# Delta rule chain: the state update finished in PSUM by an identity matmul

## Chip, cores and metric

The kernel runs on one core of a Trainium2 chip. The metric is device time of one execution in microseconds (us). The engines are called PE (TensorE, matmul), PEld (its weight loads), DVE (VectorE), ACT (ScalarE), POOL (GpSimd) and SP (SyncE, here the issuer of the DMAs). PSUM is the memory into which PE writes and from which DVE and ACT read.

## The reference, cut to what matters

Four layers; each mixes tokens and then applies a feed-forward block, over 512 tokens (256 of context, 256 latent). Token mixing has two parallel branches. The one that matters here is an RWKV-7 mixer with 8 heads of width 64, in two directions. Its state is a 64x64 matrix per head and direction:

```
sa = -einsum('vk,k->v', S, kk_t)
S  = S * w_t + sa * b_t + v_t * k_t        (decay per key channel, two outer products)
y  = einsum('vk,k->v', S, r_t)
```

The kernel computes it in chunks of 64 tokens. Within a chunk the decay is folded into keys and queries (a key is multiplied by the inverse of the decay so far, a query by the decay so far). From chunk to chunk the state, written with keys on the partitions, becomes `c * (K^T U + S)`. Here `c` is the decay over the whole chunk (one number per key channel), `K` holds the scaled keys and b vectors of the chunk, and `U` holds its values and solved vectors.

## The kernel before, in words

Nothing is emitted as it is written. Each call on `pe`, `act`, `vec`, `pool` or `dma` records a node (`Plan.add`, line 150) with its predecessors and an estimated cost (line 198). `Plan.schedule` (line 243) then orders all nodes of the whole kernel by list scheduling: each engine takes the ready node with the highest rank, and a rank is the estimated length of the longest chain behind the node plus a bias by stream. `emit` (line 338) issues everything in that order from one line, L343, so the profile is read by tile names and not by lines. Calls inside `plan.together(share)` (line 140) become one node and are issued in a row; `share` multiplies their estimated cost. Each engine works through its own instructions in the order issued.

In the mixing stage of a layer several generators (streams) run against each other (lines 1312 to 1337): for each of four head pairs `rw_pair` (preparation, line 812), `rw_solve` (a triangular inverse, line 985) and `rw_chain` (the chunk recurrence, line 1031), for each of four heads of the other branch `hg_head` (line 1140), and `gate_tiles` (line 1300). All of them draw projections through `proj` (line 521): weights are loaded as `wr`, split into two parts by ACT (`wh`) and by DVE or POOL (`wl`), and used in three matmuls into `p_ps`.

`rw_pair` writes, per direction `d` and half `s4` (chunks 0 to 3, then 4 to 7), the keys `BK` (128 partitions: two heads of 64 key channels; 512 columns a half). It takes score matmuls of them (`pz`, masked by DVE into `SC`), transposes them on PE and has ACT copy them into `BKT`. `pcs[:, d, s]` is the decay over chunk `s`, one number per partition.

`rw_chain` runs over chunks `s` = 0 to 7 of a pair; there are four pairs in each of four layers, so 128 steps, 112 of which (`s` < 7) update the state, 96 of them with an old state (`s` > 0). A step is a relay in one PSUM tile, `c_ps`, of which there is one buffer (`PSB`, line 49):

1. four matmuls of `SC` and `UV`, in which the state sits (profile: `c_ps<-UV,SC`), copied out by ACT into a part of the tile `S` (`S<-c_ps`, line 1052);
2. four matmuls by `ZA` (`c_ps<-S,AR`), copied by ACT into `UV` (two instructions, line 1059);
3. four matmuls of `BKT` and `UV` into columns 256 to 383 (`c_ps<-UV,BKT`, line 1066);
4. the state update on DVE (lines 1075 to 1087): for each direction and head into `UV` of the next chunk, 64x64, and for each direction into the tile `S`, 128x64. It reads the PSUM columns, multiplies by `pcs` and adds `S0P`, the old state already multiplied by `pcs` on POOL (line 1072). For `s` = 0 there is no old state, and the instruction only multiplies.

After chunks 2, 3, 6 and 7 outputs `y` are taken from the same PSUM tile (lines 1089 to 1112).

Of the kernel before, what the change touches and what calls it, by code (L numbers as in the profile page):

```python
# [12 lines left out]
AF = mybir.ActivationFunctionType  # L13
ALU = mybir.AluOpType
PSUM = bass.MemoryType.PSUM

P = 128
# [12 lines left out]
C = 64  # L30
# [62 lines left out]
class Plan:  # L93
# [104 lines left out]
    def cost(eng, name, out, args, kw):  # L198
# [31 lines left out]
        if name == "tensor_scalar":  # L230
            if ptr:
# [7 lines left out]
               act=dict(pe=230.0, act=145.0, vec=143.0, pool=170.0, dma=200.0),  # L239
               vec=dict(pe=245.0, act=130.0, vec=127.0, pool=130.0, dma=200.0),  # L240
               pool=dict(pe=205.0, act=72.0, vec=156.0, pool=97.0, dma=200.0))
# [112 lines left out]
def body(ctx, tc, xT, cc, ada_w, w_in, rw_lo, rw_g2, proj_a, proj_b, w_out, ffn_w1, ffn_w2,  # L354
         vecs, lbl, c_id, c_bo, c_sc, c_hg, c_sh, out, depth=4):
    nc = tc.nc
    plan = Plan(nc, tc)
    vec, act, pool, pe, dma = plan.vec, plan.act, plan.pool, plan.pe, plan.dma
# [13 lines left out]
    def st(tag, shape, dt=F32, bufs=1):  # L372
        return plan.tile(sp, shape, dt, tag, 2 if tag in B2 else bufs, tag)
# [6 lines left out]
    ident = const(c_id, name="ident")  # L380
# [17 lines left out]
    def sps(tag="s"):  # L398
        return plan.tile(pss, [P, 512], F32, tag, PSB[tag], tag + "_ps")
# [342 lines left out]
    hd = (slice(0, C), slice(C, P))  # L742

    def layer(l, pm, xs, xd, hh, hl):
# [67 lines left out]
        def rw_pair(p):  # L812
# [116 lines left out]
            for s4 in range(0, NCH, 4):  # L929
                yield lambda s4=s4: p == 0 or flags.get(("chain", p - 1), -1) >= s4 + 3  # L930
                yield ("at", par["ps"][p] + par["pn"])
                ss = slice(s4, s4 + 4)
                for h in range(0 if s4 else 2):
                    pool.memset(UV[hd[h], :, 0, h, :], 0.0)
                w = C if last and s4 == 0 else P
                for d in range(2):
                    BK, ar = BKs[d], ARt[:, d]
                    pz = [sps().rearrange("p (s c) -> p s c", s=4) for _ in range(2)]
                    with plan.together(0.55):
                        for i in range(4):  # L940
                            for h in range(2):
                                pe.matmul(pz[h][:, i, 0:w], BK[hd[h], s4 + i, :, :], ar[hd[h], s4 + i, 0:w // C, :],
                                          start=True, stop=True)
                    for h in range(2):
                        hs, psv = hd[h], pz[h]
                        vec.tensor_tensor(out=SC[:, d, ss, h, 0:w], in0=psv[:, :, 0:w],
                                          in1=scm[:, 0:w].unsqueeze(1).to_broadcast([P, 4, w]), op=ALU.mult)
                        if not EA[last]:
                            vec.tensor_tensor(out=ZA[z0, d, ss, h, :], in0=psv[hs, :, 0:C],
                                              in1=scm[hs, 0:C].unsqueeze(1).to_broadcast([C, 4, C]), op=ALU.mult)  # L950
                        pool.tensor_copy(SC[hs, d, ss, h, 0:C], ar[hs, ss, 0, :])
                        yield 1
                    ps = sps()
                    for i in range(4):
                        pe.transpose(ps[:, i * P:(i + 1) * P], BK[:, s4 + i, :, :], ident)
                    act.activation(BKT[:, d, ss, :], ps.rearrange("p (a c) -> p a c", a=4), AF.Copy)
                    yield 1
                    ps = sps()
                    for i in range(2):
                        o0 = (s4 + 2 * i) * C  # L960
                        pe.transpose(ps[:, i * P:(i + 1) * P], (vr if d else v)[:, o0:o0 + P], ident)
                    for g in range(2):
                        pv = ps[hd[g], 0:2 * P].rearrange("p (a h c) -> p a h c", a=2, h=2)
                        for h in range(2):
                            act.activation(UV[hd[1 - h], d, s4 + g:s4 + 4:2, h, :], pv[:, :, h, :], AF.Copy)
                    yield 1
# [64 lines left out]
        def rw_chain(p):  # L1031
# [12 lines left out]
            for s in range(NCH):  # L1044
                ps = sps("c")
                pu = ps[z0, 0:256]
                with plan.together():
                    for d in range(2):
                        for h in range(2):
                            pe.matmul(pu[:, (2 * d + h) * C:(2 * d + h + 1) * C], SC[:, d, s, h, 0:C],  # L1050
                                      UV[:, d, s, h, :], start=True, stop=True)
                act.activation(Rs, pu, AF.Copy)
                with plan.together():
                    for d in range(2):
                        for h in range(2):
                            pe.matmul(ps[hd[h], d * C:(d + 1) * C], ZA[z0, d, s, h, :],
                                      Rs[:, (2 * d + h) * C:(2 * d + h + 1) * C], start=True, stop=True)
                for h in range(2):
                    act.activation(UV[hd[h], :, s, h, :], ps[hd[h], 0:2 * C].rearrange("p (d c) -> p d c", d=2),
                                   AF.Copy)  # L1060
                yield 1
                if s < NCH - 1:
                    with plan.together():
                        for d in range(2):
                            for h in range(2):
                                pe.matmul(ps[hd[h], 256 + d * C:256 + (d + 1) * C],
                                          BKT[:, d, s, h * C:(h + 1) * C], UV[:, d, s, h, :], start=True, stop=True)
                    s0p = [None, None]
                    if s:
                        for d in range(2):  # L1070
                            s0p[d] = st("S0P", [P, C], bufs=2)
                            pool.tensor_scalar(out=s0p[d], in0=S[:, d, s % 4, :], scalar1=pcs[:, d, s:s + 1],
                                               scalar2=None, op0=ALU.mult)

                    def update(dst, d, r):
                        po, pc = ps[r, 256 + d * C:256 + (d + 1) * C], pcs[r, d, s:s + 1]
                        if s:
                            vec.scalar_tensor_tensor(out=dst, in0=po, scalar=pc, in1=s0p[d][r], op0=ALU.mult,
                                                     op1=ALU.add)
                        else:  # L1080
                            vec.tensor_scalar(out=dst, in0=po, scalar1=pc, scalar2=None, op0=ALU.mult)

                    for d in range(2):
                        for h in range(2):
                            update(UV[hd[h], d, s + 1, h, :], d, hd[h])
                    for d in range(2):
                        update(S[:, d, (s + 1) % 4, :], d, slice(0, P))
                    yield 1
                if s % 4 < 2 or last and s < 4:
                    flags["chain", p] = s  # L1090
                    continue
                ns = (s - 1, s) if s % 4 == 2 else (s - 3, s)
                steps = []
                for i, n in enumerate(ns):
                    sb = 3 - n if n < 4 else 11 - n
                    steps += [(0, i, 0, n), (0, i, 1, sb)] + [(1, i, 0, n)] * (n > 0) + [(1, i, 1, sb)] * (sb > 0)
                steps.sort()
                fin = {i: x for x in steps for i in (x[1],)}
                with plan.together(0.75):
                    for x in steps:  # L1100
                        st_, i, d, n = x
                        for h in range(2):
                            po = ps[hd[h], 384 + i * C:384 + (i + 1) * C]
                            if st_:
                                w, a = S[hd[h], d, n % 4, :], ARt[hd[h], d, n, 1, :]
                            else:
                                w, a = UV[:, d, n, h, :], SC[:, d, n, h, C:P]
                            pe.matmul(po, w, a[:, ::-1] if d else a, start=x == steps[0], stop=fin[i] == x,
                                      skip_group_check=True)
                st_ = ns[1] - ns[0]  # L1110
                act.activation(y.rearrange("p (n c) -> p n c", c=C)[:, ns[0]:ns[1] + 1:st_],
                               ps[:, 384:512].rearrange("p (n c) -> p n c", c=C), AF.Copy)
                flags["chain", p] = s
                yield 1
# [410 lines left out]
```

## Time and profile before

| | |
|---|---|
| median of 3 runs | 4313.35 us (4310.06 to 4324.89) |
| profiled execution, its own time | 4312.55 us |
| span of that execution (first to last instruction) | 4310.8 us |
| busy: PE, PEld, DVE | 3855.0, 3058.9, 3309.3 us |
| busy: ACT, POOL | 2149.9, 1890.7 us |
| mean granted TensorE clock | 0.932 |

A granted clock of 1.00 is TensorE at 2.4 GHz throughout, one of 0.50 at 1.2 GHz throughout. Busy PE time includes matmuls that overlap in its pipeline, so the length of a matmul group on PE is better read from the start of the group to the start of the next one. Matmuls of fp32 operands are recorded as two instructions each. Rows with `x4` merge four instructions into one line of the timeline.

### The profile page before, as it was taken

The numbers are of one execution on the slowest core, as the hardware profiler recorded it, in microseconds if no ns is written. First come the engines' busy times: TensorE is split into PE (matmuls) and PEld (weight loads), VectorE is DVE, ScalarE is ACT, GpSimd is POOL, SyncE is SP. The second block draws the span as 40 slices with busy tenths as digits, with TensorE's granted clock in tenths as the row PEclk, the third lists the DMA queues.
The fourth block names the chain that finished last, engine by engine and source line by source line (L and its number), as shares of the span: only waits on it lengthen the run. The fifth ranks groups of instructions, "written<-read, shape, count | busy, mean of one in ns | idle before, by whom it ended". The sixth has DMA issues, their size and how long they took to land.

```text
span 4310.8 us, 71511 instructions
## 1 busy us (share of the span) xinstructions
PE 3855.0 (89%) x26290; PEld 3058.9 (71%) x26290; DVE 3309.3 (77%) x5764; ACT 2149.9 (50%) x4234; POOL 1890.7 (44%) x1617
## 2 busy tenths in 40 slices
PE   7889998899988998999999889899899997788898
PEld 4666666777776666677777766677777775567798
DVE  5989979999179899668753898987676379988676
ACT  4556653433255566544333555565433255566564
POOL 1343444455433444464554243454455433244332
PEclk8889899999998898999999989899999998788999
DMA  4111137466321111363543212116354331112555
GB/s 150 57 53 48 52 122 217 138 182 177 91 85 52 59 50 55 122 186 115 159 123 107 64 38 63 43 56 221 108 164 140 108 102 45 41 51 63 170 151 160
DMA packets 661407, 451.02 MB, mean 105 GB/s; under 512 B 28224, under 2 KB 584256, under 8 KB 661056
## 3 DMA queue, kind: packets, MB, share of 16 engines
q1 hardware_dynamic: 661056, 446.44, 34.7%
q8 instruction: 207, 3.39, 0.3%
q14 instruction: 144, 1.18, 0.1%
HBM read 416.98 MB, written 29.36 MB: 104 GB/s over the span
## 4 chain that ended last, share of the span: by engine, by line
PE 42%; DVE 19%; issue 10%; POOL 5%; ACT 2%; DMA 1%; POOLq 0%; SPq 0%; DVEq 0%; ACTq 0%
PE p_ps L343 32%; POOL wl L343 4%; PE s_ps L343 4%; DVE XS L343 4%; PE c_ps L343 3%; PE g_ps L343 2%; DVE wl L343 2%; DVE S L343 2%; DVE X8b L343 1%; DVE AR L343 1%; DVE hX L343 1%; DVE UV L343 1%; DVE X8a L343 1%; DVE BK L343 1%; DVE X4c L343 1%
## 5 line engine op out<-in xcount | busy, mean ns | idle before, releaser
L343 PE MATMUL p_ps<-hh,wl 128*128 128x512 f32 (+1 forms) x2784 | 1091.0, 397 | 107.0 <-DVE wl L343 53.5
L343 PE MATMUL p_ps<-hh,wh 128*128 128x512 f32 (+1 forms) x2784 | 1073.9, 390 | 0.0
L343 PE MATMUL p_ps<-hl,wh 128*128 128x512 f32 (+1 forms) x2784 | 1066.2, 389 | 0.0
L343 ACT ACTIVATE wh<-wr 128x512 fp32r<-128x512 f32 x986 | 611.0, 622 | 860.8 <-PE p_ps L343 684.4
L343 POOL TENSOR_TENSOR wl<-wr,wh 128x512 fp32r<-128x512 f32 x487 | 674.3, 1392 | 746.9 <-ACT wh L343 517.0
L343 PEld LDWEIGHTS p_ps<-hh,wl 128*128 128x128 f32 x2784 | 543.7, 196 | 245.9 <-POOL wl L343 77.0
L343 PEld LDWEIGHTS p_ps<-hl,wh 128*128 128x128 f32 x2784 | 541.8, 195 | 97.6 <-issue 7.2
L343 PEld LDWEIGHTS p_ps<-hh,wh 128*128 128x128 f32 x2784 | 543.6, 196 | 90.7 <-issue 4.9
L343 DVE TENSOR_TENSOR wl<-wr,wh 128x512 fp32r<-128x512 f32 (+1 forms) x499 | 377.6, 762 | 99.6 <-ACT wh L343 89.9
L343 POOL TENSOR_SCALAR fn<-fn 128x512 f32<-128x512 f32 (+1 forms) x152 | 236.4, 1555 | 246.1 <-ACT fn L343 220.0
L343 POOL TENSOR_SCALAR S0P<-S,pcs 128x64 f32<-128x64 f32 x192 | 151.4, 802 | 316.8 <-DVE S L343 316.2
L343 DVE TENSOR_TENSOR fn<-fn,p_ps 128x512 f32<-128x512 f32 (+1 forms) x208 | 127.7, 615 | 162.0 <-ACT fn L343 81.2
L343 ACT ACTIVATE fn<-fn 128x512 f32<-128x512 f32 (+1 forms) x304 | 174.5, 575 | 103.2 <-POOL fn L343 98.8
L343 POOL TENSOR_TENSOR HB<-HB,HA 128x512 f32<-128x512 f32 x112 | 157.7, 1408 | 155.2 <-ACT hY L343 153.2
L343 DVE TENSOR_TENSOR XS<-XS,S 64x30 f32<-64x30 f32 (+14 forms) x480 | 203.9, 425 | 11.7
L343 DVE TENSOR_TENSOR S<-XS 64x30 f32<-64x30 f32 (+14 forms) x480 | 193.2, 402 | 11.6
L343 POOL COPY SC<-XS 64x256 f32<-64x256 f32 x128 | 67.6, 528 | 263.1 <-DVE SC L343 250.3
L343 POOL TENSOR_TENSOR HA<-HA 128x512 f32<-128x512 f32 x112 | 144.2, 1287 | 11.4 <-ACT hX L343 5.0
L343 PE MATMUL p_ps<-SC,wh 128*128 128x512 f32 (+1 forms) x440 | 144.2, 361 | 0.0
L343 DVE SCALAR_TENSOR_TENSOR UV<-c_ps,pcs,S0P 64x64 f32<-64x64 f32 x384 | 108.6, 283 | 36.7 <-PE c_ps L343 26.6
L343 ACT ACTIVATE fn<-p_ps 128x512 f32<-128x512 f32 (+1 forms) x217 | 112.2, 518 | 42.9 <-PE p_ps L343 23.6
L343 ACT ACTIVATE hY<-HB 128x512 f32<-128x512 f32 x128 | 85.0, 664 | 89.2 <-PE g_ps L343 74.5
(478 smaller groups left out, 8761.7 us busy)
## 6 DMA issues: line engine op xcount, KB each, us to landing
wr<-ffn_w SPq DMA_DIRECT2D x512, 256.0 KB, 3.1
wr<-w_in SPq DMA_DIRECT2D x408, 256.0 KB, 2.9
hq<-ada_w SPq DMA_DIRECT2D x242, 256.0 KB, 3.0
PB<-ada_w SPq DMA_DIRECT2D x110, 256.0 KB, 2.8
wr<-w_out SPq DMA_DIRECT2D x64, 256.0 KB, 3.0
gts<-fn SPq DMA_DIRECT2D x48, 256.0 KB, 2.4
wr<-proj_a SPq DMA_DIRECT2D x32, 256.0 KB, 3.9
wr<-proj_b SPq DMA_DIRECT2D x32, 256.0 KB, 3.6
```

The lines of the kernel that those rows point to most:

```text
L343: getattr(self.eng[self.on[i]], name)(*args, **kw)
```

## The change

In `rw_pair` one DVE instruction is added per direction and half: after the score matmuls have read the keys, `BK` is multiplied in place by the chunk decay. In `rw_chain` the DVE update goes. POOL still multiplies the old state by the decay, now both directions into one tile with one buffer. PE starts the accumulation with two identity matmuls that bring this tile into PSUM, and the four matmuls with `BKT` add to it. ACT copies the result into `UV` (two instructions), DVE copies it into `S` (one instruction).

```diff
                         pool.tensor_copy(SC[hs, d, ss, h, 0:C], ar[hs, ss, 0, :])
                         yield 1
+                    bk = BK[:, ss].rearrange("p s x j -> p s (x j)")
+                    vec.tensor_tensor(out=bk, in0=bk, in1=pcs[:, d, ss].unsqueeze(2).to_broadcast([P, 4, P]),
+                                      op=ALU.mult)
                     ps = sps()
                     for i in range(4):
                         pe.transpose(ps[:, i * P:(i + 1) * P], BK[:, s4 + i, :, :], ident)
...
                 if s < NCH - 1:
-                    with plan.together():
+                    if s:
+                        s0p = st("S0P", [P, 2, C], bufs=1)
+                        for d in range(2):
+                            pool.tensor_scalar(out=s0p[:, d], in0=S[:, d, s % 4, :], scalar1=pcs[:, d, s:s + 1],
+                                               scalar2=None, op0=ALU.mult)
+                    with plan.together(0.7):
+                        for h in range(2 if s else 0):
+                            pe.matmul(ps[hd[h], 256:256 + 2 * C], ident[:, hd[h]], s0p.rearrange("p d c -> p (d c)"),
+                                      start=True, stop=False, skip_group_check=True)
                         for d in range(2):
                             for h in range(2):
                                 pe.matmul(ps[hd[h], 256 + d * C:256 + (d + 1) * C],
-                                          BKT[:, d, s, h * C:(h + 1) * C], UV[:, d, s, h, :], start=True, stop=True)
-                    s0p = [None, None]
-                    if s:
-                        for d in range(2):
-                            s0p[d] = st("S0P", [P, C], bufs=2)
-                            pool.tensor_scalar(out=s0p[d], in0=S[:, d, s % 4, :], scalar1=pcs[:, d, s:s + 1],
-                                               scalar2=None, op0=ALU.mult)
-
-                    def update(dst, d, r):
-                        po, pc = ps[r, 256 + d * C:256 + (d + 1) * C], pcs[r, d, s:s + 1]
-                        if s:
-                            vec.scalar_tensor_tensor(out=dst, in0=po, scalar=pc, in1=s0p[d][r], op0=ALU.mult,
-                                                     op1=ALU.add)
-                        else:
-                            vec.tensor_scalar(out=dst, in0=po, scalar1=pc, scalar2=None, op0=ALU.mult)
-
-                    for d in range(2):
-                        for h in range(2):
-                            update(UV[hd[h], d, s + 1, h, :], d, hd[h])
-                    for d in range(2):
-                        update(S[:, d, (s + 1) % 4, :], d, slice(0, P))
+                                          BKT[:, d, s, h * C:(h + 1) * C], UV[:, d, s, h, :], start=not s,
+                                          stop=True, skip_group_check=True)
+                    new = ps[:, 256:256 + 2 * C].rearrange("p (d c) -> p d c", d=2)
+                    for h in range(2):
+                        act.activation(UV[hd[h], :, s + 1, h, :], new[hd[h]], AF.Copy)
+                    vec.tensor_copy(S[:, :, (s + 1) % 4, :], new)
                     yield 1
```

## Rows read from the trace of the kernel before

**Rows 1.** Windows: three mixing stages, and the sum over all four.
```profile
100.00:640.00 540.00, 481.79 (x4111) 359.79 (x4111) 480.18 (x925) 313.49 (x633) 220.99 (x217) 0.91 0.21 62
1210.00:1815.00 605.00, 535.29 (x4388) 408.39 (x4388) 532.46 (x1026) 348.53 (x706) 245.96 (x236) 0.90 0.20 61
2330.00:2915.00 585.00, 518.16 (x4263) 399.20 (x4262) 501.13 (x977) 338.44 (x684) 236.24 (x231) 0.91 0.19 58
...
sum 2265.00, PE 1977.97 PEld 1523.81 DVE 1980.95 ACT 1313.63 POOL 919.68; mean PE 494.49 PEld 380.95 DVE 495.24 ACT 328.41 POOL 229.92
```

**Rows 2.** Chain that ended last, 1210 to 1815 us, shares by engine and tile.
```profile
by line: PE p_ps L343 26.5%; issue 9.6%; PE s_ps L343 8.1%; DVE XS L343 8.0%; PE c_ps L343 7.0%; DVE wl L343 5.1%; PE g_ps L343 4.7%; DVE S L343 4.3%; DVE X8b L343 3.2%; DVE AR L343 2.5%; DVE hX L343 2.4%; DVE X8a L343 1.8%; DVE SC L343 1.8
```

**Rows 3.** Groups by shape, DVE: count | busy us, mean ns | idle before, releasers.
```profile
L343 DVE SCALAR_TENSOR_TENSOR UV<-c_ps,pcs,S0P 64x64 f32<-64x64 f32 x384 | 108.6, 283 | 36.7 <-PE c_ps L343 26.6 <-ACT wh L343 2.6 <-ACT he L343 0.6
L343 DVE SCALAR_TENSOR_TENSOR S<-c_ps,pcs,S0P 128x64 f32<-128x64 f32 x192 | 45.6, 279 | 2.2
L343 DVE TENSOR_SCALAR UV<-c_ps,pcs 64x64 f32<-64x64 f32 x64 | 18.1, 283 | 10.0 <-PE c_ps L343 6.6 <-ACT wh L343 2.4
L343 DVE TENSOR_SCALAR S<-c_ps,pcs 128x64 f32<-128x64 f32 x32 | 7.6, 279 | 0.5
```

**Rows 4.** Groups by shape, DVE, the nearest to the added instructions.
```profile
L343 DVE TENSOR_TENSOR SC<-s_ps,scm 128x512 f32<-128x512 f32 x112 | 76.4, 684 | 3.4 <-PE s_ps L343 2.1
...
L343 DVE TENSOR_TENSOR X8a<-X8a,X8b 128x512 f32<-128x512 f32 x32 | 27.6, 864 | 0.2
...
L343 DVE COPY SS<-g_ps 128x128 f32<-128x128 f32 x32 | 8.1, 278 | 3.1 <-PE g_ps L343 3.0
```

**Rows 5.** Groups by shape, ACT, the copy into UV.
```profile
L343 ACT ACTIVATE UV<-c_ps 64x128 f32<-64x128 f32 x256 | 69.1, 270 | 65.9 <-PE c_ps L343 61.4 <-DVE S L343 1.2
```

**Rows 6.** Timeline, one update of the last chain of layer 0: start, length.
```profile
593.37 0.45 PE L343 MATMUL c_ps<-UV,BKT 128*64 128x64 f32 x8
...
593.75 0.50 PE L343 MATMUL p_ps<-hh,wh 128*128 128x512 f32 x1
...
593.97 1.21 DVE L343 SCALAR_TENSOR_TENSOR UV<-c_ps,pcs,S0P 64x64 f32<-64x64 f32 x4 [0.35 <-PE c_ps L343]
594.09 0.60 PE L343 MATMUL g_ps<-vt,HB 128*128 128x128 f32 x4
...
594.45 0.71 PE L343 MATMUL p_ps<-hl,wh 128*128 128x512 f32 x2
...
595.21 0.47 DVE L343 SCALAR_TENSOR_TENSOR S<-c_ps,pcs,S0P 128x64 f32<-128x64 f32 x2
...
595.66 0.85 POOL L343 TENSOR_SCALAR S0P<-S,pcs 128x64 f32<-128x64 f32 x2 [6.13 <-DVE S L343]
...
595.83 0.65 PE L343 MATMUL c_ps<-UV,SC 128*64 128x64 f32 x8
...
598.76 0.45 PE L343 MATMUL c_ps<-UV,BKT 128*64 128x64 f32 x8
```

**Rows 7.** Timeline, one update of the first chain of layer 0.
```profile
236.72 0.64 PE L343 MATMUL c_ps<-UV,BKT 128*64 128x64 f32 x8
...
240.48 1.21 DVE L343 SCALAR_TENSOR_TENSOR UV<-c_ps,pcs,S0P 64x64 f32<-64x64 f32 x4
241.72 0.48 DVE L343 SCALAR_TENSOR_TENSOR S<-c_ps,pcs,S0P 128x64 f32<-128x64 f32 x2
242.10 2.19 POOL L343 TENSOR_SCALAR S0P<-S,pcs 128x64 f32<-128x64 f32 x2 [2.07 <-DVE S L343]
```

**Rows 8.** Tile S0P: ns min/median/max; last, idle time of its engines by releaser.
```profile
L343 POOL TENSOR_SCALAR S0P<-S,pcs x192: 433/542/3309, 233.1 to 4010.4; 128x64 f32<-128x64 f32 x192
...
  PE c_ps L343: 26.6, 29
```

**Rows 9.** Timeline, two readers of one PSUM tile in the last layer's tail.
```profile
4296.92 0.38 ACT L343 ACTIVATE fn<-p_ps 128x256 f32<-128x256 f32 x1 [3.18 <-PE p_ps L343]
...
4297.33 0.48 DVE L343 TENSOR_SCALAR hY<-p_ps,pr 128x256 f32<-128x256 f32 x1 [3.13 <-ACT fn L343]
```

## The prediction

> **What bounds the kernel now.** I began with the table of busy times. PE is busy for 3855.0 of 4310.8 us, but it is not the only limit, so the next view is the windows over the four mixing stages, where all of the change lies [rows 1]. There the reader is to see two engines almost equally full: PE 1978.0 and DVE 1981.0 of 2265 us (87% each), ACT at 58%, POOL at 41%, and a granted clock of about 0.9 (between the levels 1.2 and 2.4 GHz, nearer the higher). Which of two full engines limits such a stage is read from the chain that ended last in it [rows 2]. PE stands there with 26.5 + 8.1 + 7.0 + 4.7 = 46%, DVE with 8.0 + 5.1 + 4.3 + 3.2 + 2.5 + 2.4 + 1.8 + 1.8 = 29% in the lines that are listed, and 25% is left for issue time, hand-overs and small lines. So a microsecond taken off DVE is worth about 0.29 us, one put on PE costs about 0.46 us, and a relay through the chain's steps counts by about 0.25. These three weights are my estimate; one stage stands for all four.
>
> **DVE.** The change removes the whole update: 108.6 + 45.6 + 18.1 + 7.6 = 179.9 us [rows 3]. It adds 112 copies of 128x128 from PSUM. The same shape takes 278 ns, so 31 us [rows 4]. It adds 64 scalings of 128x512 in SBUF (4 pairs, 2 directions, 2 halves, 4 layers). They are not in the trace. The nearest are an fp32 product of the same shape with one operand in PSUM at 684 ns and one with both operands in SBUF at 864 ns [rows 4]: 44 to 55 us, nothing below, since they replace no instruction. I take 55, the operands being in SBUF. Net: -179.9 + 31 + 55 = -94 us, and -107 with the shorter price and 253 ns a copy (8.1 us / 32). At 0.29 that is -27 us. What a lighter DVE leaves late next is the projections and chain matmuls on PE, which have the larger weight already. The scaling stands between score matmuls and transposes. What is queued behind it on DVE is the next mask or the solver; the transposes and ACT's copy into `BKT` wait for it. `BKT` is read only in the third part of a chain step, so I give this wait no price of its own; without that cover the first update of each half waits, 32 halves by 0.86 us, 28 us at weight 0.25, 7 us.
>
> **PE.** In 96 steps two identity matmuls come ahead, fp32, 64 outputs by 128 columns: four recorded instructions. Four instructions of 128 columns take 594.45 - 594.09 = 0.36 us from start to start; the four existing matmuls, eight instructions of 64 columns, 0.38 us [rows 6]. If the two heads, which go to different halves of the array's outputs, overlapped fully it would be half, 0.18. So 17 to 36 us, of which I take 0.36 x 96 = 35, since the group in the trace has the same number of columns. At 0.46 it costs 16 us.
>
> **ACT and POOL.** ACT gains 224 copies of 0.270 us [rows 5], 60 us. What hides them is ACT's free time, 42% of the stages [rows 1]; the part that the chain sees is in the next term. Without that cover the 60 us count like the chain, about 15 us. POOL does the same 192 products as before.
>
> **The relay of a step.** Before, on a free DVE, the next matmuls start 595.83 - 593.37 = 2.46 us after the matmuls of the update: 0.60 to DVE's first instruction, 1.71 of updates, 0.15 back [rows 6]. The output tile has one buffer, so the copy into `S` must end as well. After: 0.36 (identity) + 0.60 + 0.54 (two ACT copies) + hand-over + 0.28 (DVE copy) + 0.15. How DVE and ACT stand to each other decides the hand-over, and [rows 9] shows it: two readers of one PSUM tile with no data between them, and DVE sat idle 3.13 us until ACT had ended, then began 0.03 us later. So 0.36 + 0.60 + 0.54 + 0.03 + 0.28 + 0.15 = 1.96, a gain of 0.50. On a loaded step DVE came only 240.48 - 236.72 = 3.76 us after the matmuls [rows 7], and afterwards two queues, ACT's and DVE's, lie one behind the other, so the gain there may be nothing. I take 0.3 us: 112 x 0.3 x 0.25 = -8 us; the ends are 0 and -14.
> On this the Trainium skill (PSUM — Partial Sum Buffer, section on bank collisions) speaks against the change: two engines must not touch one bank in the same 32 partitions at once, reads included, and compilers put one behind the other. By that rule, which the idle DVE of [rows 9] bears out, the sum stays as above; were the copies side by side, each step would be 0.31 us shorter still.
>
> **Sum.** -27 + 16 - 8 = -19 us against the profiled execution's 4312.55 (span 4310.8 and 1.75 around it), so 4293.5; the median of the runs lies 0.8 above, so 4294.
> The planner orders everything anew, and what an order is worth can be bounded: the three stages that run the same code leave PE idle for 58.2, 69.7 and 66.8 us [rows 1]. A spread of 11.5, so about 6 either way a stage: 12 us over four if independent, 23 if all go one way.
>
> **Rivals.**
> *PE is the bound (slower).* If PE's stretches weigh 0.8 and DVE's 0.1, because PE's queue is in order and its group grows in every step, the sum is +28 - 9 = +19: 4332. For: PE has the largest share [rows 2]. Against: DVE's 29% are stretches in which PE waits. It decides from the point where PE's weight is over 2.7 times DVE's (94 / 35); now it is 1.6.
> *The old state comes late (slower).* Before, the product `S0P` was needed only by DVE's update; DVE's idle time before those was ended by PE, never by POOL [rows 8]. Now PE itself waits for it, and projections and other heads' matmuls are queued behind. The spare time was 598.76 - 596.51 = 2.25 us in a free step [rows 6], but a pair takes 0.85 there, 2.19 in the loaded one [rows 7], and one product has taken 3.31 [rows 8]. If a quarter of the 96 steps lose 1.5 us on PE, that is +36 on -19: +17, 4330. Against: median 542 ns, so most pairs take 1.1 us. It decides from 13 steps on (19 / 1.5).
> The Trainium skill (SBUF — State Buffer, section on the two separate sides) has a rule that feeds this one: a DVE instruction with two SBUF inputs and a POOL instruction that reads SBUF exclude each other for their whole length. The removed updates had one SBUF tensor and the added scaling has two, so by the rule, which the stretch from 433 to 3309 ns agrees with, 64 new blocks reach POOL; I raise this rival from 0.10 to 0.12 for it, no more.
> *Nothing to be measured.* DVE's time is refilled at once because weight splits, solver and projections are late next, and its weight is half of what the chain shows: -14 + 16 - 8 = -6, 4307. For: both engines are equally full. Against: the saving lies in the stretch where DVE makes PE wait.
> *The copies run side by side.* 112 x 0.31 x 0.25 = 9 us and the low end of the identity cost, 8 us less: 4277. Against: [rows 9].
>
> **How the numbers follow.** Forecast 0.45, no change 0.20, PE bound 0.15, old state late 0.12, side by side 0.08. A difference of 0.3% is 13 us, about what a measurement of this kernel can tell from no change: 4300 to 4326. The forecast and its spread by order (4282 to 4306) give 0.37 faster and 0.08 same; side by side 0.08 faster; no change 0.04 faster, 0.14 same, 0.02 slower; the two slower rivals 0.24 slower, 0.03 same. Together: faster 0.49, same 0.25, slower 0.26. The low end takes DVE's net at -107 with a weight of 0.45 (all unlisted lines DVE's), 17 us of PE, 0.5 us a step and a good order: -48 + 8 - 14 - 12 = -66, 4247. The high end is above both slower rivals with a little of the bad order: 4337. The forecast's own range is 4270 to 4306.
>
> **What would show it.** DVE busy about 94 us less in all, ACT 60 more; the identity group 0.36 us from its start to the group with `BKT`; DVE's copy into `S` beginning just after ACT's second copy into `UV`; few PE idles ended by POOL `S0P`; mixing stages together some 20 us shorter, everything else alike. The prediction is wrong if DVE's lines in the chain shrink and PE's grow by as much, if PE idles for `S0P` add up to over 20 us, or if the stages move by more than the spread of the order while the counts come out as worked out here.

## The result, and the profile after

The changed kernel takes 4346.38 us (median of 4 runs, 4344.15 to 4350.16) where the kernel before took 4316.68 beside it: ratio 1.006, 95% interval 1.0044 to 1.0075. By the ratio it is slower by about 26 us (the two medians lie 30 apart) where 19 less were forecast, and it lies above the range of 4247 to 4337.

The first lines of the page of after (share of the span, instructions), against 4310.8 and PE 3855.0, DVE 3309.3, ACT 2149.9 before:

```profile
span 4343.5 us, 72016 instructions
...
PE 3886.8 (89%) x26674; PEld 3078.2 (71%) x26674; DVE 3187.3 (73%) x5265; ACT 2206.8 (51%) x4458; POOL 1868.0 (43%) x1620
```

PE is busy for 31.8 us more and idle as long as before (span less PE's busy time: 455.8, then 456.7 us), so on balance the lighter DVE has shortened no waiting of PE. The work is what was counted, and DVE came out lighter still: -122 us (forecast -94), ACT +57 (60). The groups that stand in place of [rows 3] and beside [rows 5] (busy us, mean ns | idle before, releasers):

```profile
L343 ACT ACTIVATE UV<-c_ps 64x128 f32<-64x128 f32 x480 | 129.6, 270 | 143.5 <-PE c_ps L343 98.3 <-DVE S L343 38.9
...
L343 PE MATMUL c_ps<-S0P,ident 128*64 128x128 f32 x384 | 44.3, 310 | 4.4 <-ACT UV L343 4.2
...
L343 DVE COPY S<-c_ps 128x128 f32<-128x128 f32 x112 | 32.1, 287 | 56.1 <-ACT UV L343 42.8 <-PE c_ps L343 6.7 <-ACT wh L343 1.9
...
L343 DVE TENSOR_TENSOR BK<-BK,pcs 128x512 f32<-128x512 f32 x32 | 24.0, 750 | 0.1
...
L343 DVE TENSOR_TENSOR X8b<-X8b,pcs 128x512 f32<-128x512 f32 x32 | 22.8, 713 | 1.1 <-PE s_ps L343 0.9
```

The reader is to see that 180 us of DVE became 32 + 24 + 23 = 79 (so 101 of the 122 us are the change's own lines; the rest is other DVE instructions that took less time, the 128x512 weight splits 740 ns each instead of 767), that a scaling took 713 to 750 ns, between the two prices of [rows 4], and that the new copy waits most for `ACT UV`. The program says so as well: the copy into `S` carries a wait on a count of ACT. This is the order of two readers that [rows 9] showed. The Trainium skill (PSUM — Partial Sum Buffer, section on bank collisions) says that a compiler adds such a dependency between engines on one bank, reads included; the trace agrees, with 42.8 us of that wait.

The second update in the last chain of layer 0, after, to be read beside [rows 6], which is the second of its chain too (start us, length):

```profile
592.07 0.44 PE L343 MATMUL c_ps<-S0P,ident 128*64 128x128 f32 x4
...
592.34 0.40 PE L343 MATMUL c_ps<-UV,BKT 128*64 128x64 f32 x8
...
592.78 0.27 ACT L343 ACTIVATE UV<-c_ps 64x128 f32<-64x128 f32 x1 [1.04 <-PE c_ps L343]
593.15 0.29 DVE L343 COPY S<-c_ps 128x128 f32<-128x128 f32 x1 [0.67 <-ACT UV L343]
...
593.48 0.27 ACT L343 ACTIVATE UV<-c_ps 64x128 f32<-64x128 f32 x1 [0.42 <-DVE S L343]
...
593.80 0.68 PE L343 MATMUL c_ps<-UV,SC 128*64 128x64 f32 x8
```

From the identity group to the next step it is 593.80 - 592.07 = 1.73 us, where [rows 6] took 2.46 and 1.96 was forecast. The identity group takes 0.27 of it (forecast 0.36). The three copies lie one behind the other, but in the order ACT, DVE, ACT: DVE starts 0.10 us behind ACT's first copy, and ACT's second copy has to wait for DVE's. The first line of the groups above has 38.9 us of such waits. The new order of issue brought them: DVE's copy comes last, as forecast, in 36 of the 112 updates, between ACT's two in 35, and first in 41.

The chain of waits could be followed back only over the last 23% of this execution, so [rows 2] has no counterpart. Where the time went shows in windows like those of [rows 1], here of the four whole mixing stages (each from the layer's first transfer of `xd`, or 0, to its last `od<-y`) and of what lies between them. Sums over four, kernel before, then after:

```profile
sum 2346.30, PE 2044.25 PEld 1559.47 DVE 2013.54 ACT 1354.11 POOL 923.40; mean PE 511.06 PEld 389.87 DVE 503.38 ACT 338.53 POOL 230.85
...
sum 1964.50, PE 1810.75 PEld 1499.47 DVE 1295.72 ACT 795.81 POOL 967.26; mean PE 452.69 PEld 374.87 DVE 323.93 ACT 198.95 POOL 241.82
```

```profile
sum 2333.70, PE 2043.78 PEld 1556.67 DVE 1858.36 ACT 1392.25 POOL 895.49; mean PE 510.94 PEld 389.17 DVE 464.59 ACT 348.06 POOL 223.87
...
sum 2009.80, PE 1843.01 PEld 1521.56 DVE 1328.97 ACT 814.56 POOL 972.49; mean PE 460.75 PEld 380.39 DVE 332.24 ACT 203.64 POOL 243.12
```

The mixing stages did become 12.6 us shorter. What follows them became 45.3 longer, and 32.3 of that is PE busy time: PE's work of the mixing stages was the same 2044 us although the identity matmuls had come in, so other matmuls were pushed out behind: the four stretches that follow the stages hold 9423 matmul instructions (those that start in them), 9286 before. DVE fell by 155 us in the mixing stages, and little of it was gained.

### The profile page after: what moved, and what is told of

It is laid out like the page before. It is cut to its first block, busy times and chain, and to the rows that moved or that the text cites. A ratio compares the mean times of both kernels' runs of the same rounds, so it can differ in the third digit from the quotient of the medians.

```text
span 4343.5 us, 72016 instructions
## 1 busy us (share of the span) xinstructions
PE 3886.8 (89%) x26674; PEld 3078.2 (71%) x26674; DVE 3187.3 (73%) x5265; ACT 2206.8 (51%) x4458; POOL 1868.0 (43%) x1620
## 5 line engine op out<-in xcount | busy, mean ns | idle before, releaser
L343 DVE TENSOR_TENSOR wl<-wr,wh 128x512 fp32r<-128x512 f32 (+1 forms) x498 | 364.3, 735 | 143.9 <-ACT wh L343 138.1
L343 POOL TENSOR_SCALAR S0P<-S,pcs 128x64 f32<-128x64 f32 x192 | 118.6, 632 | 285.7 <-DVE S L343 271.7
L343 ACT ACTIVATE UV<-c_ps 64x128 f32<-64x128 f32 x480 | 129.6, 270 | 143.5 <-PE c_ps L343 98.3
L343 POOL COPY SC<-XS 64x256 f32<-64x256 f32 x128 | 76.8, 600 | 287.1 <-DVE SC L343 280.9
L343 DVE TENSOR_TENSOR hX<-hX,hq 128x512 f32<-128x512 f32 x128 | 103.9, 812 | 34.3 <-ACT hX L343 32.9
```

The lines of the kernel that those rows point to most:

```text
L343: getattr(self.eng[self.on[i]], name)(*args, **kw)
```

## The experiments

The planner issued nearly everything in a new order, so the parts had to be separated from it. In the kernels "in the order of before" the planner plans the kernel before; only when a node's turn to be issued comes are other instructions put in its place. Each cut of code shows the lines that matter, with comments added; the rest of the edit is left out.

```
 for _, i in self.when:
-    for name, args, kw in self.nodes[i].calls:
-        getattr(self.eng[self.on[i]], name)(*args, **kw)
+    put(i)    # what it needs first; then alt[i] if there is one, else its own calls
```

All are given against runs of the kernel before on the same chip, with the ratio's 95% interval and the difference at 4318 us.

**The parts in the order of before.** The whole change:

```
+plan.alt[n - 6 + h] = [("act", "activation", (UV[hd[h], :, s + 1, h, :], new[hd[h]], AF.Copy), {})]
+plan.alt[n - 2] = [("vec", "tensor_copy", (S[:, :, (s + 1) % 4, :], new), {})]
+# ahead of the keys' matmuls: two of ident by s0t; ahead of the first mask: BK times pcs on DVE
```

> The whole change (identity matmuls, scaled keys, old state tile of both directions, ScalarE and VectorE copies), but every instruction is issued in the order that the planner wrote for the kernel before; only the replaced instructions differ. Order theory (the planner's new order costs what was lost, the edit itself does not): at or below the kernel before, ratio 0.993 to 1.001 (4286 to 4320 us); VectorE busy about 100 us less, TensorE busy about 35 us more, TensorE idle about 30 us or more less. TensorE-bound theory (the added 35 us of identity matmuls count in full and the relief of VectorE is worth nothing): ratio 1.006 to 1.009, about 4345 us, TensorE idle as before (440 us in the eight stages).

Measured: 4340.28 us, ratio 1.0051 (1.0033 to 1.0068), +22 us. So the order theory fell: without any new order the change costs nearly all that it costs with it (+26; the intervals overlap), and PE is idle for 451 us, 456 before. PE-bound was left, and the next runs took it apart.

```
+plan.alt[g] = [("pe", "matmul", (ps[hd[h], 256:256 + 2 * C], ident[:, hd[h]], ident),
+                dict(start=True, stop=True, skip_group_check=True)) for h in range(2)]
+plan.alt[g] += [("pe",) + c for c in plan.nodes[g].calls]
```

> The kernel before in its own order, plus two identity matmuls (128x64 <- 128x128) in each of the 48 updates, which the keys' matmuls then overwrite: 96 more TensorE instructions of about 0.36 us by the forecast, nothing else. TensorE-bound theory: the 35 us count in full, +30 to +38 us (ratio 1.007 to 1.009). Forecast's weight for TensorE in the chain of waits (0.46): +16 us (1.004). Order theory: between the two, since here nothing is given back.

Measured: 4344.13 us, 1.0057 (1.0042 to 1.0072), +25 us: between forecast and full price. (There are 96 such updates and not 48; the 0.36 us are for a pair of identity matmuls.) In this run's trace the time from the start of the identity matmuls to the start of the keys' matmuls adds up to 27.7 us, so a microsecond put on PE here cost about 0.9.

```
-if s:    # the two matmuls of ident by s0t, in full_old_order
+if False:
```

> The whole change in the order of the kernel before, without the identity matmuls: the old state is left out of the update, so part of the recurrence is not computed. TensorE then does what it did before, VectorE 90 to 120 us less. TensorE-bound theory: the time of the kernel before (ratio 0.998 to 1.002). Forecast's weights (VectorE 0.29 of 94 us, relay 8 us): -35 us, ratio 0.992. The difference to the run with the identity matmuls is the price of those in this place: 35 us by the TensorE-bound theory, 16 us by the forecast.

Measured: 4319.77 us, 1.0000 (0.9991 to 1.0009). Neither theory's reason holds: the time is the PE-bound one, but the next run showed that two large terms cancel in it.

```
+self.pre[m] = [("vec", "tensor_tensor", (), dict(out=bk, in0=bk, in1=pcs, op=ALU.mult))]
+# m: the first of the two masks; pcs is broadcast along the columns
```

> The kernel before in its own order, plus the 64 VectorE scalings of the keys (in one kernel with the old update, so the decay enters twice; the output changes, the work does not). VectorE gets some 47 us more (64 x about 0.73 us). TensorE-bound theory: within 0.1% of the kernel before. Forecast's weight for VectorE (0.29): +14 us (ratio 1.003).

Measured: 4358.81 us, 1.0092 (1.0078 to 1.0107), +40 us for 48 us of DVE. Both theories missed. That made the site theory: DVE's time counts by where it lies. It leaned on two windows of before in layer 0, up to the first chain and between the second and the third (us, then busy PE, PEld, DVE, ACT, POOL, each with its instructions; PE clock):

```profile
110.00:227.10 117.10, 94.18 (x650) 73.03 (x648) 109.14 (x186) 64.05 (x120) 34.12 (x32) 0.87 0.17 50
...
403.90:484.90 81.00, 70.76 (x648) 54.19 (x643) 79.06 (x126) 54.97 (x105) 38.10 (x33) 0.94 0.20 60
```

Here DVE is full: 93% and 98%. But these two are among the fullest. The 16 stretches from the first update of a chain to its last, and then the 12 between two chains of a layer, add up in the kernel before to:

```profile
sum 778.30, PE 713.44 PEld 533.00 DVE 682.69 ACT 441.32 POOL 375.41; mean PE 44.59 PEld 33.31 DVE 42.67 ACT 27.58 POOL 23.46
...
sum 807.90, PE 703.10 PEld 536.31 DVE 706.48 ACT 493.80 POOL 335.54; mean PE 58.59 PEld 44.69 DVE 58.87 ACT 41.15 POOL 27.96
```

DVE is busy for 88% of the first and 87% of the second, and 24 of the 64 scalings of this run lie inside a chain's stretch. So how full DVE is does not tell the two places apart.

**Copies alone, and the scaling elsewhere.** In the first, the scaling and the identity matmuls are left out of full_old_order; in the others the scaling is on another engine:

```
-plan.both.append((masks, [("vec", "tensor_tensor", (), kw)], early[d], after))
-if s:
+if False:
-act.activation(BKT[:, d, ss, :], ps.rearrange("p (a c) -> p a c", a=4), AF.Copy)
+act.activation(BKT[:, d, ss, :], ps.rearrange("p (a c) -> p a c", a=4), AF.Copy, scale=1e-9)
```

> The kernel before in its own order with only the copies exchanged (two ScalarE copies and one 128x128 VectorE copy in place of six VectorE instructions): neither identity matmuls nor scaling of the keys, so old state and decay are left out, and the keys are copied out with a factor 1e-9 to keep the numbers small (same instructions). VectorE 150 us less than before. Site theory (VectorE's weight is about 0.85 in the building of the heads, where the scaling stands, and 0.27 in the chain): the runs so far give no_ident minus scale_only = -39 us for the copies, so 4280 us, ratio 0.991. Theory of no worth (VectorE's relief in the chain is worth nothing, and the scaling's price was its place in the queue): ratio 0.999 to 1.001.

Measured: 4288.02 us, 0.9925 (0.9912 to 0.9937), -32 us. The copies gain 32 of the 39 us that the site theory gave them, and the scaling on top of them costs 32 (from this run to no_ident_old_order).

```
+calls = [("act", "activation", (bk[:, i], bk[:, i], AF.Copy), dict(scale=pcs[:, d, s4 + i:s4 + i + 1]))
+         for i in range(4)]
```

> The whole change in the order of before, with the scaling of the keys as four ScalarE copies of 128x128 with a factor for each partition (256 instead of 64 VectorE instructions), issued just ahead of the transposes. ScalarE gets 256 x 0.27 us = 69 us more, VectorE 47 us less than in full_old_order (4340 us). Site theory: minus 39 us for VectorE, plus nothing to a quarter of ScalarE's 69 us: 4301 to 4319 us, ratio 0.996 to 1.000. If the scaling's price is the wait that it puts ahead of the transposes, whatever engine does it: as full_old_order, ratio 1.004 to 1.006.

Measured: 4338.02 us, 1.0038 (1.0024 to 1.0051), +16 us. A miss: 6 us came back, not 39, and the intervals of the two runs overlap. Each of the 256 took 388 ns, not 270; they overlap one another, and 81 us of busy time went onto ACT (groups of this run):

```profile
L356 ACT ACTIVATE X8b<-X8b,pcs 128x128 f32<-128x128 f32 x128 | 40.6, 390 | 0.1
...
L356 ACT ACTIVATE BK<-BK,pcs 128x128 f32<-128x128 f32 x128 | 40.5, 387 | 0.0
```

```
+calls = [("pool", "tensor_tensor", (), dict(out=bk, in0=bk, in1=pcs, op=ALU.mult))]
```

> As full_scale_act, with the scaling as one GpSimd instruction of 128x512 (64 of them), which the trace of before does not show; from GpSimd's 128x64 scaling (0.43 us) at most eight times that, 3.5 us, so up to 220 us on GpSimd, 44% busy before. Site theory: 4301 us if GpSimd hides it (ratio 0.996); if GpSimd's old-state scalings come late behind it, up to that of full_old_order (1.005) or above.

Measured: 4364.45 us, 1.0107 (1.0092 to 1.0121), +46 us, although one instruction took only about 1.08 us:

```profile
L356 POOL TENSOR_TENSOR BK<-BK,pcs 128x512 f32<-128x512 f32 x32 | 35.1, 1097 | 0.9
...
L356 POOL TENSOR_TENSOR X8b<-X8b,pcs 128x512 f32<-128x512 f32 x32 | 33.9, 1058 | 0.4
```

The site theory's lower numbers held for neither ACT nor POOL. The second theory's range for ACT begins at 1.004, inside the interval. For POOL the first had allowed more than 1.005 if the old-state products come late; but PE has no wait for `s0t`, the tile of those products, in this run. It waits for the scaled keys, ahead of their transposes (idle before, releasers):

```profile
L361 PE MATMUL s_ps<-ident,X8b 128*128 128x128 f32 x128 | 24.5, 304 | 32.4 <-POOL X8b L356 29.1 <-DVE XS L361 3.0
L361 PE MATMUL s_ps<-ident,BK 128*128 128x128 f32 x128 | 22.7, 301 | 29.8 <-POOL BK L356 29.8
```

That is 62 us ahead of the transposes, where the run with the scaling on ACT has 28 and the kernel before 13.

```
+for i in (n - 2, n - 1):    # the two copies into S
+    plan.alt[i] = [("vec",) + c for c in plan.nodes[i].calls] * 2
```

> The kernel before in its own order, with both state copies of VectorE in each of the 112 updates done twice (224 more VectorE instructions of 0.28 us, 63 us; same result): VectorE time added in the chain instead of in the building of the heads. Site theory: weight 0.27, +17 us, ratio 1.004. One weight for all of VectorE, as the 64 scalings had it (39 us for 47): +52 us, ratio 1.012.

Measured: 4382.08 us, 1.0141 (1.0123 to 1.0160), +61 us for 64 us of DVE. So the site theory fell too, in its second half: added to the chain, DVE's time counts in full as well. What PE waits for says why (PE's waits for `c_ps <- DVE S`: us, times, longest). Before, then extra_in_chain, copies_only_old_order, after:

```profile
PE c_ps L343 <- DVE S L343: 36.7, 38, 3.9
```
```profile
PE c_ps L356 <- DVE S L356: 88.9, 92, 5.5
```
```profile
PE c_ps L356 <- DVE S L356: 14.7, 17, 2.2
```
```profile
PE c_ps L343 <- ACT UV L343: 13.5, 26, 1.5
PE c_ps L343 <- DVE S L343: 11.3, 13, 3.4
```

Doubling the copies lengthened this wait by 52 us, of a price of 61. Removing 147 us of DVE could shorten it by 36.7 at the most; copies_only took 22 off it and gained 32. PE's other waits for DVE, 228 us before, did not shrink with the lighter DVE (231 in copies_only). That this one row bounds the gain fits these numbers, but no run shows it by itself. What differs is then not the stretch of the kernel but the direction: time put on DVE costs 0.8 and 0.95 of its length in these two runs, time taken off returns 0.2.

**What became of the freed DVE time.**

```
-plan.alt[n - 2] = [("vec", "tensor_copy", (S[:, :, (s + 1) % 4, :], new), {})]
+plan.alt[n - 2] = [("act", "activation", (S[:, :, (s + 1) % 4, :], new, AF.Copy), {})]
```

> As copies_only_old_order (4288 us, ratio 0.9925; no old state, no decay), with the 128x128 state copy on ScalarE too, so that VectorE has no part in the update: VectorE 32 us less again and without its 109 us of waiting for ScalarE's UV copies, ScalarE 112 x 0.29 = 32 us more. If the relief of VectorE is lost in that wait: 4255 to 4275 us, ratio 0.985 to 0.990. If only the length of the hand-over counts (and VectorE's time in the chain is worth nothing by itself): 0.991 to 0.994.

Measured: 4286.83 us, 0.9921 (0.9908 to 0.9935), like copies_only and inside the second number. DVE's longest waits, copies_only and then copies_s_act; the first of these was 89.9 us before:

```profile
DVE wl L356 <- ACT wh L356: 112.1, 153, 3.7
DVE S L356 <- ACT UV L356: 109.2, 78, 5.2
```
```profile
DVE wl L356 <- ACT wh L356: 165.6, 176, 4.6
```

The time that DVE no longer works it waits for ACT: first for the `UV` copies, and when these waits were taken away, for the weight splits, whose first half is ACT's. ACT, which was off the path, became the engine that DVE waits for most. PE's own waits for `wl` of DVE stayed the same (56.2 us before, then 54.9 and 56.0).

```
+calls = [("vec",) + c for i in (n - 2, n - 1) for c in plan.nodes[i].calls]
+calls.append(("act", "activation", (UV[hd[h], :, s + 1, h, :], S[hd[h], :, (s + 1) % 4, :], AF.Copy), {}))
```

> Another form of the update, with the whole computation and neither identity matmuls nor scaling: VectorE writes the new state S for both directions (2 x 0.28 us, with decay and old state as before), ScalarE copies UV from S (2 x 0.27 us); order of before. VectorE 448 x 0.28 = 125 us less, ScalarE 224 x 0.27 = 60 us more; UV is ready 1.15 us after the keys' matmuls plus one more hand-over, as against 1.13 us before. If VectorE's time in the chain is worth 0.2 to 0.3 by itself: 4283 to 4295 us, ratio 0.991 to 0.994. If only the length of the hand-over counts: 4316 to 4340 us, ratio 0.999 to 1.005.

Measured: 4307.59 us, 0.9969 (0.9957 to 0.9981), -13 us, between the two theories. It is faster than both kernels: DVE relieved, PE and the making of the keys untouched.

```
-plan.both.append((masks, [("vec", "tensor_tensor", (), kw)], early[d], after))
-act.activation(BKT[:, d, ss, :], ps.rearrange("p (a c) -> p a c", a=4), AF.Copy)
+act.activation(BKT[:, d, ss, :], ps.rearrange("p (a c) -> p a c", a=4), AF.Copy, scale=1e-9)
```

> Copies and identity matmuls in the order of before, without the scaling of the keys (the decay of the new part is left out; keys copied out with a factor 1e-9 as in copies_only_old_order). If the parts add up: copies -32 us, identity matmuls +20 to +25 us, so 4308 to 4313 us, ratio 0.997 to 0.999. If the identity matmuls hide where VectorE isn't loaded with the scaling: 0.9925 to 0.995.

Measured: 4312.66 us, 0.9983 (0.9971 to 0.9994), -7 us. The parts add up: -32 + 25. The identity matmuls cost 25, 25 and 22 us on three backgrounds, the scaling 40, 32 and 29; by the intervals each is known to some 9 us, so these differences are not resolved. The profiles show in what form each is paid. PE's idle time, 456 us before, is 435 with the copies, 491 with the scaling and 462 with the identity matmuls, which also keep PE busy for 25 us more: copies and scaling count mainly through PE's waiting, the identity matmuls mainly as work of PE.

**Is the scaling's price DVE's time, or its place?**

```
+if h:
+    n = len(plan.nodes) - 1    # the mask SC<-s_ps,scm
+    plan.alt[n] = [("vec",) + c for c in plan.nodes[n].calls] * 2
```

> The kernel before in its own order, with 64 of its 128 mask multiplications of the scores (mostly 128x512, 0.68 us) done twice: about 41 us of VectorE at the place where the scaling of the keys stands, but with nothing for the transposes of the keys to wait on; same result. If the scaling's price is VectorE's time in the building of the heads: +26 to +41 us, ratio 1.006 to 1.0095. If it is the wait that it puts ahead of the transposes: 0.999 to 1.002.

Measured: 4350.58 us, 1.0079 (1.0066 to 1.0093), +34 us for 42 us of masks with no transposes waiting on them: PE's idle time ahead of the transposes is 17 us, 13 before and 30 in scale_only. So DVE's time alone costs as much a microsecond (0.8) as the scaling did.

```
-m = min(masks, key=place.get)
+m = min(after, key=place.get)    # the four transposes
```

> The whole change in the order of before, the scaling on VectorE as in full_old_order (1.0051) but issued just ahead of the transposes, behind the masks. If VectorE's time is the price: 1.004 to 1.006 again. If it was that the scaling stands ahead of the masks and holds them: 0.996 to 1.001.

Measured: 4366.93 us, 1.0115 (1.0099 to 1.0130), +50 us, above both numbers. Ahead of the masks was the better place: here the transposes wait more. PE's idle time ahead of them, full_old_order, then full_scale_late:

```profile
L363 PE MATMUL s_ps<-ident,X8b 128*128 128x128 f32 x128 | 24.4, 302 | 13.5 <-DVE SC L363 10.9 <-DVE S L363 2.4
L363 PE MATMUL s_ps<-ident,BK 128*128 128x128 f32 x128 | 20.9, 285 | 17.6 <-DVE SC L363 17.0 <-DVE hdec L363 0.2
```
```profile
L361 PE MATMUL s_ps<-ident,X8b 128*128 128x128 f32 x128 | 25.0, 309 | 36.4 <-DVE X8b L356 36.1
L361 PE MATMUL s_ps<-ident,BK 128*128 128x128 f32 x128 | 22.9, 303 | 37.3 <-DVE BK L356 37.3
```

So the place in the queue has a price as well: 43 us more of this waiting, 28 us more of time. This also answers for full_scale_act and full_scale_pool, which had the late place: against this run ACT saved 33 us, and POOL, with 62 us of waiting instead of 74, next to nothing.

**The price of an order.** Noise on the planner's ranks, the same three lines in both kernels:

```
+noise = np.random.default_rng(1).uniform(0.0, 250.0, N)
+rank = [r + float(x) for r, x in zip(rank, noise)]
 ready = {e: [] for e in self.ENG}
```

> The kernel before with random noise (0 to 250 ns) added to the planner's ranks: the same instructions in another order. It prices a new order by itself, which the forecast put at up to 12 us either way. If the kernel's order was fitted closely: 4330 to 4360 us (ratio 1.003 to 1.010); if the order is worth little: 0.998 to 1.002.

> The kernel before with the same noise, seed 2. If its order is fitted and any other costs: as seed 1, ratio 1.007 to 1.015. If seed 1 was a bad draw: 0.998 to 1.005.

> The changed kernel with random noise (0 to 250 ns) on the planner's ranks, seed 1. If its order of issue is as good as an order fitted to it, noise makes it worse as it did the kernel before (+49 us): about 4395 us, ratio 1.017. If its order is already a chance one: 4330 to 4365 us, ratio 1.002 to 1.010.

> The changed kernel with the noise on the planner's ranks, seed 2. The kernel before lies at 4369 and 4376 us under such noise, the changed one at 4369 with seed 1. If the change costs nothing in a chance order: 4360 to 4380 us (ratio 1.010 to 1.015). If it costs its own parts there too (21 us in the order of before): 4385 to 4400 us, ratio 1.016 to 1.020.

> As after_j2, seed 3: ratio 1.010 to 1.015 if the change costs nothing in a chance order, 1.016 to 1.020 if it costs its own parts.

| kernel | us | ratio | interval |
|---|---|---|---|
| before, seed 1 | 4368.99 | 1.0115 | 1.0099 to 1.0130 |
| before, seed 2 | 4375.76 | 1.0135 | 1.0119 to 1.0150 |
| after, seed 1 | 4369.16 | 1.0122 | 1.0103 to 1.0141 |
| after, seed 2 | 4362.81 | 1.0110 | 1.0093 to 1.0127 |
| after, seed 3 | 4365.04 | 1.0112 | 1.0097 to 1.0127 |

The same work in an order shaken by a quarter of a microsecond takes 50 and 58 us more (the first lies above both ranges written down for it). The changed kernel with seed 1 lies between its two; with seeds 2 and 3 it is where the change costs nothing. Under noise the means are 1.0125 and 1.0115, so no price of the change can be told from two and three draws. The order of before is better than both of its shaken ones, and the prices of the parts hold in that order. Noise costs the changed kernel less, some 22 to 27 us on top of its own 26, which would fit a kernel that gave up part of a fitted order; that reading is argued. Whether its own constants, set anew, would bring it below the kernel before was not tried.

## Why the prediction was wrong

**The step that failed** is the sentence "a microsecond taken off DVE is worth about 0.29 us", applied to the net of -94 us. It gave time taken out and time put in one price. Taken out of the chain, 147 us gave 32, with the relay (0.22 a microsecond; forecast 0.29 of 149 and 8, so 51). Put in, time cost far more wherever it was tried: the 48 us of scalings 29 to 40 (0.6 to 0.8; forecast 0.29 of 55, so 16), 42 us of masks 34, 64 us of copies in the chain 61. By those the change's two terms are +8 to -3 instead of -35, which is most of the miss of 45. Netting them in one number hid this. The profile had one half of it: 36.7 us of PE's waits for the copy into `S`. The price of an addition stood in no row of it; DVE's busy share, 88% in the chains and 87% between them, gives a reason why added time finds little cover, and that reason is argued. That the scaling's wait needed no price was right only for the place that it had: in full_scale_late the wait ahead of the transposes went from 31 to 74 us.

**PE.** The groups were counted rightly, but both factors were off, in opposite directions. 0.36 us a step was taken and 0.28 measured (27 us in all, not 35), and a microsecond cost 0.8 to 0.9 and not 0.46. That 16 us were forecast and 22 to 25 measured is in part luck.

**The relay.** 1.96 us from the identity group to the next step was forecast for a free step, and 1.73 came out. Over the 112 updates the mean from the update's first matmul to the next step's was 3.98 us before, 3.72 with the copies alone in the order of before, and 3.54 in after (starts in the timelines); 0.3 us of gain were forecast. The weight was off: over all 16 chains the time from the first update to the last (the starts of the first and last `c_ps<-UV,BKT` in the timeline, summed) fell from 778 to 747 us with the copies alone, while everything else stayed within 5 us. So the gain of the copies is the shorter relay, at nearly its full length, and the rest of DVE's relief gave nothing that can be seen. In after the chains fell to 724.

**The order.** "12 us over four if independent" was read from PE's idle time in three stages of one order. All three share that order's fit; shaking it costs 50 us and more. For the changed kernel it came to little: +26 in its own order, +22 in that of before, not resolved. But the order took its own way to it: the chains are 54 us shorter, the stretches between them and ahead of a layer's first one 15 and 19 longer, and those from a layer's last chain to the next layer's first transfer of `xd`, or the end, 52.

**The rivals.** "PE is the bound" came nearest with 4332, and half for the right reason: its weight of 0.8 for PE is what the identity matmuls cost. Its 0.1 for DVE is refuted by scale_only (40 us for 48), and copies_only shows that DVE's relief is worth something. "The old state comes late" is refuted: among PE's waits after there is none for `S0P`, and the tile's rows, to be read beside [rows 8] (min/median/max ns), show no one waiting:

```profile
L343 POOL TENSOR_SCALAR S0P<-S,pcs x192: 433/458/2836, 235.8 to 4036.1; 128x64 f32<-128x64 f32 x192
...
who waited for it (us, times):
```

Its median fell from 542 to 458 ns, so the port rule by which I raised this rival (the Trainium skill, SBUF — State Buffer, section on the two separate sides) had no visible effect on these products here; no run separates it. "The copies run side by side" is refuted by the waits of `S` for `ACT UV` and of `UV` for `DVE S`.

## What to carry to other kernels

Price what is taken away and what is put in separately. Here time taken off DVE was worth what it shortened the relay by, and the row of PE's waits that it could end (36.7 us) was a fair guide to the most; time put on DVE cost 0.6 to 0.95 of its length at every place tried. Shares of a chain that ended last were no exchange rate between engines. And where a list scheduler orders the kernel, shake its order before reading anything into one per cent: compare parts in a fixed order, and whole kernels over several orders.

## What was unexpected of the hardware

In one stretch, time added on DVE showed up as a lower clock of PE. In scale_only the stretch between the first and the second chain of layer 0 grew from 70.80 to 76.10 us. The same 549 matmuls took 66.06 us at a granted clock of 0.98, almost all at 2.4 GHz, and with the scaling 71.04 at 0.91, partly at 1.2; 66.06 x 0.98 / 0.91 is 71.1. So nearly all of this stretch's growth is PE at a lower clock. Ahead of it, in the first chain, PE was busy for 86% in both, at 0.83 before and 0.76 with the scaling. Which idle time of PE did it the trace doesn't show, and it is one profile each. It is no account of the scaling's whole price: over the whole execution the granted clock is 0.932 before and 0.931 in scale_only, and PE's idle time grew by 35 us. Before, then scale_only, both stretches in turn:

```profile
227.10:275.40 48.30, 41.66 (x399) 30.22 (x397) 45.33 (x113) 24.50 (x58) 29.66 (x31) 0.83 0.15 44
275.40:346.20 70.80, 66.06 (x549) 50.01 (x548) 59.04 (x101) 40.04 (x77) 21.85 (x20) 0.98 0.22 66
```
```profile
229.30:280.50 51.20, 44.22 (x398) 32.03 (x396) 46.76 (x115) 24.84 (x59) 31.15 (x31) 0.76 0.13 39
280.50:356.60 76.10, 71.04 (x549) 53.53 (x548) 62.13 (x106) 40.00 (x77) 22.79 (x20) 0.91 0.21 64
```

A copy of 128x128 within SBUF with a factor for each partition took ACT 388 ns from start to end (317 ns of busy time each, since they overlap), where 64x128 from PSUM takes 270; from `S` in uv_from_s the 64x128 copy took 309:

```profile
L356 ACT ACTIVATE UV<-S 64x128 f32<-64x128 f32 x224 | 69.1, 309 | 134.6 <-DVE S L356 131.8
```
